# Two layers of a hybrid decoder: other PSUM banks for the first unit, outputs before gate products, and splits at other places

## The chip, the core and the metric

The kernel runs on one core of a Trainium2 chip, as one launch. The metric is the device time of a run in microseconds (us). The kernel before takes 1011.71 us, the median of three runs from 1011.68 to 1012.67.

## The reference, cut to what matters

256 tokens of 1024 channels go through two layers. Each layer adds half a SwiGLU, then a mixer, then half a SwiGLU. The mixer of the first layer is a diagonal state-space layer (S5), that of the second is block attention (MoBA; with 256 tokens, one block, it is causal attention). All is float32.

```python
def swiglu(h, w_gate, w_up, w_down):
    return (jax.nn.silu(h @ w_gate) * (h @ w_up)) @ w_down          # D_FF = 2816

def s5_mixer(h, ...):
    u = (h @ w_in)
    ...                                    # y: output of the linear recurrence over u, plus d_skip * u
    g = jax.nn.gelu(y)
    g = g * jax.nn.sigmoid(g @ w_glu)
    return g @ w_out

for layer in range(2):
    h = h + 0.5 * swiglu(rms_norm(h, ffn_norm[layer, 0]), ...)
    h = h + mixer[layer](rms_norm(h, mix_norm[layer]))
    h = h + 0.5 * swiglu(rms_norm(h, ffn_norm[layer, 1]), ...)
```

## The kernel before

**Phases.** The six phases run one after another on one stream of weights: `f00`, `s5`, `f01`, `f10`, `moba`, `f11`. `ffn` (L414) is `f00`, `ffn_w` (L513) the other three SwiGLUs.

**Products.** Each float32 product is made of three products of parts: a value is split into a high part (`whi`, `xh`) and the low rest (`wlo`, `xl`), and TensorE sums high x high, high x low and low x high into one bank of PSUM (`mm3`, L377 to L380; in `ffn_w` L531 to L533; in `glu` L1059 to L1061). The activations' parts are the tile `xa`.

**The weight stream** (`Stream`, L36). The weights come in units of 128 x 2048 float32, loaded by SP's queue into three raw buffers. A unit has two halves. `split` (L72) makes the high part of the next half on ScalarE (L81, with the norm's gain L87) and the low part on VectorE (L82, with gain L88, two pieces of 512 each); after the second half the raw buffer is free, and the load of the unit three places on is issued. There are nine slots for split halves (`HB`). `pump(n)` splits up to n halves if a slot and a raw buffer are there; `get` splits on the spot what is not split yet; `release` gives a slot back.

**The order of work is the order of the program.** Every engine runs its instructions in the order in which the Python code emits them (`manual_schedule`), and waits at each for its semaphores. So the place of a `pump` in the code is the place of the split in ScalarE's and VectorE's queues.

**PSUM.** Eight banks: two named pM (`psM`, sums of the gate and up products), two named pR (`psR`, transposes and small sums), and pA0 to pA3 (`psA`, the four sums of the down products; in S5 also the sums of the gate products, `glu`, and of the output products, `so`). A bank is taken again once the last reader of its tile before is done.

**f00.** For each of eleven units j of 256 columns, `gu(j, t)` makes gate and up sums of token tile t (eight steps k, of three products each), `gated` (L457) takes the Silu of the gate half on ScalarE into `sg`, pumps, and multiplies on VectorE into `act` (L463); `tr` transposes `act` (L476), `dn` adds to the down sums. The first unit, `gu0` (L438), goes through k with both token tiles in turn, since the inputs still arrive, and has its two sums in the two pM banks. The next unit's `gu(1, 0)` takes a pM bank again.

**S5.** `w_in` makes u in four parts. Then, for each of eight groups b: `t1` (L967) products, `rot` on VectorE (complex rotation and two scans) and GpSimd (L996 to L999), which gives `hr`; `y_out(b)` (L1016) sums the outputs in a pR bank, Gelu on ScalarE (`yg`, L1030), two transposes on VectorE (`gs`, L1033); `g_tr(b)` (L1036) transposes on TensorE into a pR bank, from which ScalarE and VectorE write the parts of g (low part L1046); `glu(b)` (L1048) adds group b's part of g @ w_glu to the four pA banks and pumps at set places. Within the last `glu`, `gate(i)` (L1069) takes the sigmoid (L1072), multiplies (L1074) and makes high and low parts (L1076, L1077). `so(b, t, n)` are the output products, `boundary` (L354) ends them, with `finish` (L352) adding the sums to h and `prep` transposing and splitting h for the next phase (L314, L316, L317). The last `prep` of a phase stands in the next one, at step k = 2 of its first unit (`entry_hooks`).

The loop that the change touches, with the groups' order (L1098):

```python
for b in range(3, NB):
    glu(b - 3)
    y_out(b)
    if b + 3 < NB:
        t1rot(b + 3)
    g_tr(b - 1)
```

Of the kernel before, what the change touches and what calls it, by code (L numbers as in the profile page):

```python
# [10 lines left out]
F32 = mybir.dt.float32  # L11
# [104 lines left out]
def trunk_kernel(ctx: ExitStack, tc, x, ffn_norm, ffn_w_gate, ffn_w_up, ffn_w_down, mix_norm,  # L116
# [10 lines left out]
    fp = ctx.enter_context(tc.tile_pool(name="ffn", bufs=2))  # L127
# [3 lines left out]
    def psM():  # L131
        return pp.tile([128, 512], F32, name="pM", tag="M", bufs=2)

    def psR():
        return pp.tile([128, 512], F32, name="pR", tag="R", bufs=2)

    def psA(i):
        return pp.tile([128, 512], F32, name=f"pA{i}", tag=f"A{i}", bufs=1)
# [129 lines left out]
    st = Stream(nc, units, rp, hp)  # L268
# [108 lines left out]
    def mm3(o, xh, xl, wh, wl, start, stop):  # L377
        mm(o, xh, wh, start=start, stop=False)  # L378
        mm(o, xh, wl, start=False, stop=False)  # L379
        mm(o, xl, wh, start=False, stop=stop)  # L380
# [33 lines left out]
    def ffn(tag, nxt, hooks, fill):  # L414

        V = nc.vector
        acc = [None] * 4
        AT, AC = {}, {}

        def gu(j, t, hooks):  # L420
            us = [where[tag, "g", j, a] for a in range(2)]
            ps = psM()
            ts = slice(t * 128, t * 128 + 128)
            for k in range(8):
                for fn in hooks.get(k, ()):
                    fn()
                fill(0.7)
                wh, wl = st.get(us[k // 4], (k % 4) // 2)
                c = slice((k % 2) * 512, (k % 2) * 512 + 512)
                mm3(ps, X["h"][:, k, ts], X["l"][:, k, ts], wh[:, c], wl[:, c], k == 0, k == 7)  # L430
                if k % 2:
                    if k < 7 and (j, t, k) != (L, 1, 5):
                        st.pump()
                    if t == 1:
                        st.release(us[k // 4], (k % 4) // 2)
            gated(j, t, ps)

        def gu0():  # L438

            us = [where[tag, "g", 0, a] for a in range(2)]  # L440
            pt = [psM() for t in range(2)]
            for q in range(4):
                u = us[q // 2]
                for t in range(2):
                    for f in hooks.get((q, t), ()):
                        f()
                    ts = slice(t * 128, t * 128 + 128)
                    for k in (2 * q, 2 * q + 1):
                        fill(0.7)
                        wh, wl = st.get(u, q % 2)  # L450
                        c = slice((k % 2) * 512, (k % 2) * 512 + 512)
                        mm3(pt[t], X["h"][:, k, ts], X["l"][:, k, ts], wh[:, c], wl[:, c], k == 0, k == 7)
                st.release(u, q % 2)
            for t in range(2):
                gated(0, t, pt[t])

        def gated(j, t, ps):  # L457
            sg = fp.tile([128, 256], F32, name="sg", bufs=1)
            nc.scalar.activation(sg, ps[:, 0:256], AF.Silu, scale=Rr[t])
            if (j, t) != (L, 1):  # L460
                st.pump()
            AC[t] = fp.tile([128, 256], F32, name="act", bufs=2)
            V.scalar_tensor_tensor(AC[t], ps[:, 256:512], Rr[t], sg, op0=OP.mult, op1=OP.mult)  # L463

        def tr(j, t):
            if t == 0:
                AT[j] = []
                for i, n in enumerate(("ah", "al")):
                    o = AO[2 * i + j % 2]
                    a2 = fp.tile([128, 640], F32R, name=n, bufs=2)  # L470
                    AT[j].append(a2[:, o:o + 512].rearrange("p (f c) -> p f c", c=256))
            ps = psR()
            pv = ps[:, 0:256].rearrange("p (f c) -> p f c", c=128)
            a = AC.pop(t)
            for f in range(2):
                nc.tensor.transpose(pv[:, f, :], a[:, f * 128:(f + 1) * 128], ident)  # L476
            ah, al = (x[:, :, t * 128:t * 128 + 128] for x in AT[j])
            nc.scalar.activation(ah, pv, AF.Copy)
            V.tensor_tensor(al, pv, ah.bitcast(F32), op=OP.subtract)

        def dn(j, f):
            u = where[tag, "d", j]
            for t in range(2):
                for n in range(2):
                    if j == 0 and f == 0:
                        acc[2 * t + n] = psA(2 * t + n)
                    bank_mm(acc, t, n, *AT[j], u, [f], j == 0 and f == 0, False)
                    fill(0.7)
                if t == 1:
                    st.release(u, f)  # L490
                st.pump()

        L = NJ - 1
        for j in range(NJ):
            if j == 0:
                gu0()
                continue
            gu(j, 0, {3: [lambda: tr(0, 0)], 6: [lambda: tr(0, 1)]} if j == 1 else {6: [lambda: tr(j - 1, 1)]})
            if j > 1:
                dn(j - 2, 1)  # L500
            gu(j, 1, {6: [lambda: tr(j, 0)]})
            if j:
                dn(j - 1, 0)

        def part(j, f):
            return lambda t, n: bank_mm(acc, t, n, *AT[j], where[tag, "d", j], [f], False, (j, f) == (L, 1))

        boundary(nxt, [part(L - 1, 1), part(L, 0), part(L, 1)], acc, 0.5, lambda: tr(L, 1))
        st.release(where[tag, "d", L - 1], 1)
        for i in range(2):  # L510
            st.release(where[tag, "d", L], i)
# [429 lines left out]
    def s5(nxt, entry):  # L941
# [65 lines left out]
        def t1rot(b):  # L1007
            t1ld(b)
            rot_ld(b)
# [6 lines left out]
        def y_out(b):  # L1016
            tb = TB.pop(b)
            v2 = tb[:, 0:1024].rearrange("p (i q c) -> p i q c", i=2, c=128)
            v3 = tb[:, 1024:1536].rearrange("p (q c) -> p q c", c=128)
            ps = psR()  # L1020
            hr = H.pop(b)
            for q in range(4):
                o = ps[:, q * 64:(q + 1) * 64]
                mm(o, v3[:, q, :], U[:, 4 * b + q, :, :], start=True, stop=False)
                mm(o, v2[:, 0, q, :], hr[:, 0, q, :], start=False, stop=False)
                mm(o, v2[:, 1, q, :], hr[:, 1, q, :], start=False, stop=True)
            if b + 3 < NB:
                ld_b(b + 3)
            yg = wp.tile([128, 4, 2, 32], F32, name="yg", bufs=1)
            nc.scalar.activation(yg.rearrange("p q t c -> p (q t c)"), ps[:, 0:256], AF.Gelu_apprx_tanh)  # L1030
            gs = wp.tile([128, 2, 4, 32], F32, name="gs", bufs=2)
            for t in range(2):
                V.transpose(gs[:, t], yg[:, :, t, :])  # L1033
            GS[b] = gs
# [13 lines left out]
        def glu(b, after=None):  # L1048

            u = where["glu", b // 2]  # L1050
            if b == 0:
                for i in range(4):
                    acc[i] = psA(i)
            gh, gl = GT["h"][:, b, :], GT["l"][:, b, :]
            wh, wl = st.get(u, b % 2)
            for o in range(8):
                d = acc[o // 2][:, (o % 2) * 256:(o % 2) * 256 + 256]
                c = slice(o * 128, o * 128 + 128)
                mm(d, wh[:, c], gh, start=b == 0 and o % 2 == 0, stop=False, skip_group_check=True)  # L1059
                mm(d, wh[:, c], gl, start=False, stop=False, skip_group_check=True)  # L1060
                mm(d, wl[:, c], gh, start=False, stop=b == NB - 1, skip_group_check=True)  # L1061
                if o == 7:
                    st.release(u, b % 2)
                if o == 3 and b < 7 or o == 7 and b in (5, 6):
                    st.pump()
                if after is not None and o % 2 == 1:
                    after(o // 2)
# [28 lines left out]
        t1rot(5)  # L1096
        g_tr(1)
        for b in range(3, NB):  # L1098
            glu(b - 3)
            y_out(b)  # L1100
            if b + 3 < NB:
                t1rot(b + 3)
            g_tr(b - 1)
# [8 lines left out]
        for b in range(2):  # L1112
            for t in range(2):
                for n in range(2):
                    so(b, t, n)
                if t == 1:
                    for i in range(2):
                        st.release(where["so", b], i)
                st.pump()
            st.pump()  # L1120

        boundary(nxt, [lambda t, n: so(2, t, n), lambda t, n: so(3, t, n, True)], acc, 1.0)
        for b in (2, 3):
# [171 lines left out]
    def fill(dt):  # L1295
        slot[0] += dt
        if slot[0] > 9.0:
            next(tab, None)
# [123 lines left out]
```

## Time and profile before

| | |
|---|---|
| runs | 1011.68, 1011.71, 1012.67 us |
| the profiled execution's own time | 1011.32 us |
| its span, from the first to the last instruction | 1009.5 us |
| mean granted TensorE clock | 0.998 |
| VectorE busy | 707.0 us (70%) |
| ScalarE busy | 574.4 us (57%) |
| GpSimd busy | 167.3 us (17%) |
| f00 | to about 228 us |
| S5 | about 228 to 335 us |
| f01's first unit and first down products | about 335 to 360 us |

In rows of the timeline, the first number is the start in us from the start of the span, the second the length in us; then engine, line, operation, `out<-in`, shapes, and the count of instructions merged into the row. In brackets stands how long the engine was idle before the row and what released it. Rows of the waits give engine, tile and line that waited, who released it, the total in us, how often, and the longest. A row of the windows gives a stretch and its length, the busy time of each engine with its instructions, the granted clock (1.00 is full), the DMA engines' share and GB/s.

### The profile page before, as it was taken

What the parts mean: (1) busy time and instruction counts of PE and PEld (TensorE: products, weight loads), DVE (VectorE), ACT (ScalarE), POOL (GpSimd) and SP (SyncE); (2) the same over time, 40 slices, a digit from 0 to 9 for tenths busy, and PEclk for the clock granted to TensorE, in tenths of its full rate; (3) what the DMA queues carried; (4) which work ended last, traced back from release to release, by engine and by line L of the source; (5) the groups of instructions that cost most, each with busy time, mean ns of one, the idle gap of its engine ahead of it and who ended that gap; (6) DMA issues with size and microseconds to landing.
All of it is one profiled execution on the core that took longest, in us unless ns stands there. A gap on an engine that the chain in (4) does not pass through costs nothing.

```text
span 1009.5 us, 16571 instructions
## 1 busy us (share of the span) xinstructions
PE 993.0 (98%) x6393; PEld 889.0 (88%) x6393; DVE 707.0 (70%) x1144; ACT 574.4 (57%) x1040; POOL 167.3 (17%) x330
## 2 busy tenths in 40 slices
PE   8999999999999999999999999999999999999998
PEld 6788888888997889999989999999888899999997
DVE  4799676857967677666657766666689667766662
ACT  5656778744335656555546555553788655555551
POOL 4981222113740100000000000000342010000000
PEclk9999999999999999999999999999999999999999
DMA  8886776876735467565626665645354456656531
GB/s 258 231 271 225 240 255 216 280 294 234 269 117 196 139 211 248 168 208 168 208 84 209 235 222 169 208 168 172 117 164 139 159 173 210 223 195 208 169 126 42
DMA packets 137535, 197.59 MB, mean 196 GB/s; under 512 B 16288, under 2 KB 109040, under 8 KB 137200
## 3 DMA queue, kind: packets, MB, share of 16 engines
q1 hardware_dynamic: 133088, 183.16, 54.6%
q0 software_dynamic: 3616, 12.66, 3.2%
q8 instruction: 50, 0.82, 0.3%
q10 hardware_dynamic: 752, 0.71, 0.3%
q14 instruction: 29, 0.24, 0.1%
HBM read 182.84 MB, written 13.66 MB: 195 GB/s over the span
## 4 chain that ended last, share of the span: by engine, by line
PE 87%; DVE 5%; issue 3%; POOL 2%; ACT 2%; ACTq 0%; POOLq 0%; DVEq 0%
PE pM L533 12%; PE pM L531 12%; PE pM L532 12%; PE pA L379 9%; PE pA L380 9%; PE pA L378 9%; PE pM L378 5%; PE pM L379 5%; PE pM L380 5%; DVE wlo L82 1%; PE pR L314 1%; POOL qrs L287 1%; PE pR L863 1%; DVE zo L992 1%; PE pR L843 1%
## 5 line engine op out<-in xcount | busy, mean ns | idle before, releaser
L531 PE MATMUL pM<-xa,whi 128*128 128x256 f32 x1056 | 295.7, 280 | 1.9 <-ACT whi L87 1.9
L533 PE MATMUL pM<-xa,wlo 128*128 128x256 f32 x1056 | 294.8, 279 | 0.3 <-DVE wlo L88 0.3
L532 PE MATMUL pM<-xa,whi 128*128 128x256 f32 x1056 | 294.8, 279 | 0.0
L88 DVE SCALAR_TENSOR_TENSOR wlo<-raw,gT,whi 128x512 fp32r<-128x512 f32 x328 | 228.0, 747 | 71.2 <-ACT whi L87 71.1
L82 DVE TENSOR_TENSOR wlo<-raw,whi 128x1024 fp32r<-128x1024 f32 x156 | 193.0, 1252 | 57.5 <-ACT whi L81 56.2
L87 ACT ACTIVATE whi<-raw,gT 128x512 fp32r<-128x512 f32 x328 | 213.5, 711 | 19.1 <-PE pA L380 14.1
L531 PEld LDWEIGHTS pM<-xa,whi 128*128 128x128 f32 x1056 | 198.5, 188 | 4.4 <-ACT whi L87 2.1
L532 PEld LDWEIGHTS pM<-xa,whi 128*128 128x128 f32 x1056 | 198.5, 188 | 2.5
L533 PEld LDWEIGHTS pM<-xa,wlo 128*128 128x128 f32 x1056 | 198.5, 188 | 0.5 <-DVE wlo L88 0.5
L81 ACT ACTIVATE whi<-raw 128x1024 fp32r<-128x1024 f32 x156 | 160.9, 1054 | 21.1 <-DMA raw<-in_ffn_w_up_dram 6.1
L378 PE MATMUL pA<-whi,ah 128*128 128x512 f32 x352 | 138.9, 395 | 0.3 <-ACT whi L81 0.3
L379 PE MATMUL pA<-wlo,ah 128*128 128x512 f32 x352 | 137.8, 391 | 0.8 <-DVE wlo L82 0.8
L380 PE MATMUL pA<-whi,al 128*128 128x512 f32 x352 | 137.7, 391 | 0.0
L378 PE MATMUL pM<-whi,xa 128*128 128x512 f32 x304 | 126.5, 416 | 2.3 <-DVE act L463 1.9
L546 ACT ACTIVATE sg<-gr 128x256 f32<-128x256 f32 x66 | 27.6, 418 | 165.4 <-DVE gr L543 165.4
L379 PE MATMUL pM<-wlo,xa 128*128 128x512 f32 x304 | 119.8, 394 | 1.7 <-DVE wlo L82 1.6
L380 PE MATMUL pM<-whi,xa 128*128 128x512 f32 x304 | 119.7, 394 | 0.0
L329 POOL TENSOR_TENSOR ms<-ss 128x1 f32<-128x1 f32 x10 | 1.9, 194 | 479.5 <-ACT sq L326 479.5
L380 PEld LDWEIGHTS pA<-whi,al 128*128 128x128 f32 x352 | 66.1, 188 | 14.3
L379 PEld LDWEIGHTS pA<-wlo,ah 128*128 128x128 f32 x352 | 66.2, 188 | 12.4 <-DVE wlo L82 1.1
L378 PEld LDWEIGHTS pA<-whi,ah 128*128 128x128 f32 x352 | 66.1, 188 | 12.0 <-ACT whi L81 0.5
L543 DVE TENSOR_TENSOR gr<-pM,rrow 128x512 f32<-128x512 f32 x66 | 45.5, 689 | 39.8 <-PE pM L533 39.7
(248 smaller groups left out, 1264.1 us busy)
## 6 DMA issues: line engine op xcount, KB each, us to landing
raw<-in_ffn_w_down_dram SPq DMA_DIRECT2D x44, 1024.0 KB, 5.1
raw<-in_ffn_w_gate_dram SPq DMA_DIRECT2D x80, 512.0 KB, 3.7
raw<-in_ffn_w_up_dram SPq DMA_DIRECT2D x80, 512.0 KB, 4.9
raw<-in_moba_w_qkv_dram SPq DMA_DIRECT2D x12, 1024.0 KB, 5.1
TB<-dB SPq DMA_DIRECT2D x8, 768.0 KB, 6.4
raw<-in_ffn_w_gate_dram SPq DMA_DIRECT2D x16, 256.0 KB, 4.5
raw<-in_ffn_w_up_dram SPq DMA_DIRECT2D x16, 256.0 KB, 4.7
dB<-tt POOLq DMA_DIRECT2D x16, 256.0 KB, 5.1
```

What stands on the lines that cost most here:

```text
L81: nc.scalar.activation(hi, r, AF.Copy)
L82: nc.vector.tensor_tensor(lo, r, hi.bitcast(F32), op=OP.subtract)
L87: nc.scalar.activation(hi[:, c], r[:, c], AF.Identity, scale=g)
L88: nc.vector.scalar_tensor_tensor(lo[:, c], r[:, c], g, hi[:, c].bitcast(F32), op0=OP.mult, op1=OP.subtract)
L378: mm(o, xh, wh, start=start, stop=False)
L379: mm(o, xh, wl, start=False, stop=False)
L380: mm(o, xl, wh, start=False, stop=stop)
L531: mm(o, a, xh, start=k == 0 and i == 0, stop=False, skip_group_check=True)
L532: mm(o, a, xl, start=False, stop=False, skip_group_check=True)
L533: mm(o, b, xh, start=False, stop=k == 7, skip_group_check=True)
L543: V.tensor_tensor(gr, ps.rearrange("p (i c) -> p i c", i=2), Rr["row"][:, None, :].to_broadcast([128, 2, 256]), op=OP.mult)
L546: nc.scalar.activation(sg, gr[:, 0, :], AF.Silu)
```

## The change

Three things are changed; what is computed stays the same.

- In f00's first unit the two sums go to the banks pA0 and pA2 in place of pM's. The two gated rows follow each other without a split between, and two splits follow them. `sg` becomes a part of a tile of 512 columns with two buffers, under the tag of the tile `gr`.
- In S5's loop `y_out(b)` stands ahead of `glu(b - 3)`.
- `glu` pumps a second time at b = 3, 4, 5 in place of 5, 6. In the first two blocks of `so`, each token tile is followed by `pump(2)`, in place of `pump()` with one more `pump()` at the end of the block.

```diff
@@ gu0
-            pt = [psM() for t in range(2)]
+            pt = [psA(2 * t) for t in range(2)]
...
             for t in range(2):
-                gated(0, t, pt[t])
-
-        def gated(j, t, ps):
-            sg = fp.tile([128, 256], F32, name="sg", bufs=1)
+                gated(0, t, pt[t], 0)
+            st.pump(2)
+
+        def gated(j, t, ps, pumps=1):
+            sg = fp.tile([128, 512], F32, name="sg", tag="gr", bufs=2)[:, 0:256]
             nc.scalar.activation(sg, ps[:, 0:256], AF.Silu, scale=Rr[t])
             if (j, t) != (L, 1):
-                st.pump()
+                st.pump(pumps)
             AC[t] = fp.tile([128, 256], F32, name="act", bufs=2)
             V.scalar_tensor_tensor(AC[t], ps[:, 256:512], Rr[t], sg, op0=OP.mult, op1=OP.mult)
@@ glu
-                if o == 3 and b < 7 or o == 7 and b in (5, 6):
+                if o == 3 and b < 7 or o == 7 and b in (3, 4, 5):
                     st.pump()
@@ s5
         for b in range(3, NB):
+            y_out(b)
             glu(b - 3)
-            y_out(b)
             if b + 3 < NB:
                 t1rot(b + 3)
             g_tr(b - 1)
@@ s5, the blocks of so
                 if t == 1:
                     for i in range(2):
                         st.release(where["so", b], i)
-                st.pump()
-            st.pump()
+                st.pump(2)
```

## The prediction

> **What bounds the kernel now.** I read the page's first part, then the waits of TensorE, then the clock by stretches, then the timelines of TensorE, ScalarE and VectorE round each long wait that the change touches.
>
> ```profile
> PE 993.0 (98%) x6393; PEld 889.0 (88%) x6393; DVE 707.0 (70%) x1144; ACT 574.4 (57%) x1040; POOL 167.3 (17%) x330
> ```
>
> ```profile
> PE pM L378 <- DVE act L463: 1.9, 1, 1.9
> PE pM L531 <- ACT whi L87: 1.9, 1, 1.9
> ...
> PE pA L379 <- DVE wlo L82: 1.1, 2, 0.8
> PE pA L378 <- DVE xa L1076: 1.0, 1, 1.0
> ...
> PE pA L1060 <- DVE xa L1046: 0.9, 1, 0.9
> ```
>
> TensorE is busy for 98% of the span, and the change alters no product. It can win only what TensorE stands still or runs slow. The five rows are that: 6.8 us, at five places, all of them in the first unit of f00, in S5's second half and in the first units of f01.
>
> A wait costs more than its bracket, which counts from a modelled end. These rows give the difference:
>
> ```profile
> 309.31 0.28 PE L1060 MATMUL pA<-xa,whi 128*128 128x256 f32 x1
> 309.43 0.28 PE L1061 MATMUL pA<-xa,wlo 128*128 128x256 f32 x1
> 310.73 0.47 PE L378 MATMUL pA<-whi,xa 128*128 128x512 f32 x1 [1.02 <-DVE xa L1076]
> ...
> 317.94 0.50 PE L379 MATMUL pA<-wlo,xa 128*128 128x512 f32 x1 [0.35 <-DVE wlo L82]
> ```
>
> Starts are 0.12 us apart, lengths are 0.28: each product overlaps the next by 0.16 us, and a wait loses that overlap too. So 310.73 lost 1.18 us and 317.94 lost 0.51. (A 512-column product takes twice the 0.12, 0.23 us, and its 0.39 overlaps by the same 0.16.)
>
> **Part 1, f00's first unit: sums in pA, gated rows ahead of the splits.**
>
> ```profile
> 24.28 0.40 PE L380 MATMUL pM<-whi,xa 128*128 128x512 f32 x1
> 26.62 0.47 PE L378 MATMUL pM<-whi,xa 128*128 128x512 f32 x1 [1.94 <-DVE act L463]
> 26.93 0.46 PE L379 MATMUL pM<-wlo,xa 128*128 128x512 f32 x1
> ```
>
> ```profile
> 23.40 0.47 ACT L459 ACTIVATE sg<-pM,rr 128x256 f32<-128x256 f32 x1 [2.10 <-PE pM L380]
> 23.77 1.05 ACT L81 ACTIVATE whi<-raw 128x1024 fp32r<-128x1024 f32 x1
> ```
>
> ```profile
> 24.85 1.23 DVE L82 TENSOR_TENSOR wlo<-raw,whi 128x1024 fp32r<-128x1024 f32 x1 [1.82 <-ACT whi L81]
> 26.00 0.47 DVE L463 SCALAR_TENSOR_TENSOR act<-pM,rr,sg 128x256 f32<-128x256 f32 x1
> ```
>
> Now the next unit waits for a bank of pM, which the gated row of t = 0 frees at 26.47, since it stands on VectorE behind the split's low part. With the sums in pA that wait is gone. But the same edit moves the split that unit 1 needs for k = 0 and 1 behind both Silus on ScalarE, and the second Silu waits for TensorE's last product: 24.28 + 0.40 = 24.68, read about 0.1 later. One instruction of ScalarE follows the Silu by 23.77 - 23.40 = 0.37. So the high part starts at 24.78 + 0.37 = 25.15 and ends at 26.20 (1.05), the low part runs from 26.23 to 27.46 (1.23). TensorE starts one product at 26.25 and stops again: the second takes the low part, at 27.5 where it was 26.93. The stall is not removed, it is 0.57 us longer, with a new cause. Behind the waiting product stands all of unit 1. What the wait then does to the clock is the unknown:
>
> ```profile
> 24.00:26.70 2.70, 0.76 (x4) 0.32 (x4) 1.62 (x2) 0.93 (x2) 2.25 (x6) 1.00 1.09 256
> 26.70:30.50 3.80, 3.80 (x10) 2.57 (x11) 2.46 (x3) 2.25 (x3) 3.32 (x7) 0.55 0.17 18
> ```
>
> After the idle 1.94 us the granted clock is 0.55 for 3.8 us: ten products in 3.80, 0.38 each where 0.23 is usual, a loss of 1.5 us. After the change TensorE idles 1.57 + 0.8 us with one product between, more than now, so I take the slow stretch to stay and set +0.5 us (the start shifts by 0.57, and a slow stretch that ends at a fixed time would give a tenth back). Were it to go, the part would be worth 0.57 - 1.5 = -0.9. Bounds: -0.9 to +0.6.
>
> The Trainium skill (TensorE: Matmul & The Clock Gate, section "Why this matters for your kernels") asks for no idle gaps over about 3 us between bursts and says that one idle window takes the clock back to half. By that rule neither 1.94 us now nor the two shorter gaps after would cost clock. The trace shows 0.55 after 1.94 us, so I follow the row; what the rule would give is the second rival.
>
> The pA banks are free in time: the entry's transposes use them, and the down products' first write comes two units later. The tile sg moving to two larger buffers adds no instruction. I set both at nothing; the cover is those two units, and without it the down products' first write would wait up to the 0.47 us of a gated row.
>
> **Part 2, the loop of S5: y_out(b) ahead of glu(b - 3).**
>
> ```profile
> 267.25 0.36 PE L1059 MATMUL pA<-xa,whi 128*128 128x256 f32 x1
> 268.55 0.38 PE L1060 MATMUL pA<-xa,whi 128*128 128x256 f32 x1 [0.94 <-DVE xa L1046]
> ```
>
> Today glu(0) issues one product and waits for g_tr(0)'s low part (L1046). The outputs put there instead seem to fill that hole, but y_out(3) takes its sums in one of the two banks of pR, and the last two were given to g_tr(0) and g_tr(1): it needs g_tr(0)'s, whose last reader is the same L1046. So TensorE waits until 268.55 all the same, and the one product that it did ahead (0.2 us to the next start) is done later: +0.2. Bounds: +0.1 to +0.3. In the later rounds no wait stands now, and the order of rounds is unchanged. VectorE gets each round's transposes of yg ahead of the split in place of behind it, which shifts rot(6) and rot(7) by about 0.1. On SP the loads of TB now go ahead of the raw loads. All are needed rounds later: nothing.
>
> **Part 3, pumps.** In glu the extra pumps sit at b = 3, 4, 5 in place of 5, 6, so there is one more; each block of so pumps four in place of three. No split is added, they come earlier. Counting the calls: all four halves of the first two so units are split ahead of the gates (three now), and at f01's start four of its halves are ready in place of one.
>
> ```profile
> 306.09 1.99 ACT L81 ACTIVATE whi<-raw 128x1024 fp32r<-128x1024 f32 x2
> 307.98 1.07 ACT L1072 ACTIVATE sg<-pA 128x512 f32<-128x512 f32 x2
> ```
>
> ```profile
> 307.16 2.36 DVE L82 TENSOR_TENSOR wlo<-raw,whi 128x1024 fp32r<-128x1024 f32 x2 [1.82 <-ACT whi L81]
> 309.44 0.68 DVE L1074 TENSOR_TENSOR gf<-gf,sg 128x512 f32<-128x512 f32 x1
> 310.16 0.43 DVE L1076 CAST xa<-gf 128x512 fp32r<-128x512 f32 x1
> 310.62 0.69 DVE L1077 TENSOR_TENSOR xa<-gf,xa 128x512 fp32r<-128x512 f32 x1
> ...
> 316.67 5.76 DVE L82 TENSOR_TENSOR wlo<-raw,whi 128x1024 fp32r<-128x1024 f32 x5
> ```
>
> (a) At the gates two splits stand ahead of gate(0). With one of them gone (2.36 / 2 = 1.18 on VectorE), gate(0) starts at 308.3, its cast ends at 309.5, its low part at 310.2. TensorE ends glu(7) at 309.55, so its first two products run and the third waits a few hundredths: -1.14 of the 1.18.
> (b) The second half of so(1) is one of the five splits from 316.67 on, and 317.94 waited for it. It is done ahead of the gates now: -0.51.
> (c) The start of f01:
>
> ```profile
> 336.31 0.60 PE L314 MATMUL pR<-cst,h 128*128 128x128 f32 x4
> 338.81 0.38 PE L531 MATMUL pM<-xa,whi 128*128 128x256 f32 x1 [1.91 <-ACT whi L87]
> ...
> 339.60 0.38 PE L533 MATMUL pM<-xa,wlo 128*128 128x256 f32 x1 [0.29 <-DVE wlo L88]
> ```
>
> ```profile
> 337.58 0.69 DVE L317 TENSOR_TENSOR xa<-pR,xa 128x512 fp32r<-128x512 f32 x1 [1.16 <-ACT xa L316]
> ```
>
> The second half of f01's first unit is split only when TensorE asks for it, behind prep(1, 1) on ScalarE. These waits cost 1.91 + 0.29 + 2 x 0.16 = 2.52. Split before, they go; late next is prep itself: the products for k = 4 would come at 336.75 + 12 x 0.12 = 338.2, and their low part of x ends at 338.27. I leave 0.1: -2.4.
> (d) The first down products:
>
> ```profile
> 355.21 0.28 PE L533 MATMUL pM<-xa,wlo 128*128 128x256 f32 x1
> 355.75 0.50 PE L378 MATMUL pA<-whi,ah 128*128 128x512 f32 x1 [0.26 <-ACT whi L81]
> 357.01 0.50 PE L379 MATMUL pA<-wlo,ah 128*128 128x512 f32 x1 [0.76 <-DVE wlo L82]
> ```
>
> Starts at 355.33 and 355.56 without waits, at 357.01 with them: 1.45 lost, because the down weights' split comes late. Three halves ahead, it is done a unit sooner: -1.45. Further on both orders run into the nine slots and pump alike, so nothing more is won.
>
> What hides the extra splits: three more halves (six low parts of 0.7 us) stand on VectorE between the gates and the end of so, where this row shows it idle for 3.13 us:
>
> ```profile
> 326.89 0.69 DVE L352 SCALAR_TENSOR_TENSOR h<-pA,h 128x512 f32<-128x512 f32 x1 [3.13 <-PE pA L380]
> ```
>
> ```profile
> raw<-in_ffn_w_up_dram SPq DMA_DIRECT2D x16, 256.0 KB, 4.7
> ```
>
> The gates end 1.1 earlier, one split is out, so four so splits end at 320.4 and eight half parts of 0.69 at 325.9. The finish (L352) comes due at 326.89 - 1.14 - 0.51 + 0.2 = 325.4. It is up to 0.5 late, and TensorE has other products of so to do meanwhile: nothing, up to 0.5.
>
> **The sum:** 0.5 + 0.2 - 1.14 - 0.51 - 2.4 - 1.45 = -4.8 us. The profiled execution took 1011.32 (span 1009.5 and 1.8 round it), which gives 1006.5; the median of the runs lies 0.4 above it: 1006.9.
>
> **Rivals.**
> 1. As forecast, but the clock holds in f00 (the rule above). For it: 2.4 us of idle is cut in two by a product. Against it: a single gap of 1.94 sufficed. 1006.9 - 1.4 = 1005.5.
> 2. The stalls at f01's start only move. Were the early splits in so to cost as much at the finish and at prep as they save, (c) and (d) would be gone: 1011.7 + 0.5 + 0.2 - 1.65 = 1010.8, which is no change. For it: the finish is already at the edge. Against it: the idle 3.13 us. Half of it is a case of its own: 1008.8.
> 3. Slower, by the queue: the second raw of f01 can be loaded only when so(2)'s second half is split, at 318.05, four transfers over 1.4 us, each landing 4.7 us on: 324.2, high parts to 325.5, low parts to 326.2. VectorE is in order, so the finish stands behind a wait for this DMA, and with it the boundary. Beyond a landing of about 4.4 us each us costs one. It decides from a landing of 4.4 + 4.8 = 9.2 us on; at 12 us the time is 1006.9 + 7.6 = 1014.5. For it: the low parts do stand ahead of the finish. Against it: 4.7 is the median of sixteen.
>
> **How the numbers follow.** Forecast 0.54 (own range 1006.0 to 1007.8), clock holds 0.15, half of rival 2 0.13, rival 2 0.11, rival 3 0.07. About 0.2%, 2 us, is what a measurement tells from no change: faster 0.82, same 0.11, slower 0.07. The range runs from the clock's case less 0.6, 1004.9, to the half case plus 0.8, 1009.6.
>
> **What would show it.** Part 1: the wait of the first L378 in pM names ScalarE's high part, and a second wait in L379 names the low part; the clock round 27 to 30 us decides the first rival. Part 2: the wait on L1046 stands at an L1024. Part 3: no wait on L1076, on L87 at f01's start or on the first down weights. It is wrong if finishes in S5's boundary wait, or if the waits at f01 keep their length.

## The result, and the profile after

| | us, median | lowest to highest | runs |
|---|---|---|---|
| before | 1012.6 | 1011.41 to 1014.65 | 8 |
| changed | 1008.93 | 1008.61 to 1010.5 | 8 |

The ratio is 0.9964, 95% interval 0.9953 to 0.9975: 0.36% faster, 3.7 us, where 4.8 were forecast. The profiled execution of the changed kernel was the slowest of its eight, 1010.5 us with a span of 1008.7, so its trace shows a smaller gain than the runs; what is dear in it is the clock, as the rows below show. Lines 456 to 1119 have moved down by one, so L1046 is now L1047.

First TensorE's waits in the changed kernel: engine, tile and line that waited, who released it, us in total, how often, the longest.

```profile
PE pA L379 <- DVE wlo L82: 1.6, 2, 0.8
PE pM L378 <- ACT whi L81: 1.5, 1, 1.5
PE pR L1025 <- issue: 1.1, 1, 1.1
...
PE pM L379 <- DVE wlo L82: 0.9, 2, 0.8
PE pR L314 <- DVE h L352: 0.8, 1, 0.8
```

Gone are the waits on the gate's cast (L1076), on the high part at f01's start (L87) and those of f01's down products. The row pA L379 is gu0's own waiting for its first weights, which stood under pM before and now goes under the bank's new name. New are three: the high and low part in pM (part 1), y_out (L1025) and a finish (L352).

f00's first unit, TensorE's timeline and the stretch after it (busy time by engine, then granted clock, DMA share, GB/s):

```profile
26.20 0.50 PE L378 MATMUL pM<-whi,xa 128*128 128x512 f32 x1 [1.51 <-ACT whi L81]
27.46 0.69 PE L379 MATMUL pM<-wlo,xa 128*128 128x512 f32 x1 [0.76 <-DVE wlo L82]
```

```profile
26.70:30.50 3.80, 3.04 (x7) 2.38 (x8) 3.12 (x3) 1.34 (x2) 3.49 (x5) 0.62 0.31 30
```

The two waits name the two parts of one split, at 26.20 and 27.46, and the mean clock of the stretch after them is 0.62.

S5's loop, TensorE and VectorE, and the clock by stretches:

```profile
267.75 0.39 PE L1043 MATMUL pR<-cst,gs 128*128 128x128 f32 x2
269.24 0.41 PE L1025 MATMUL pR<-U,TB 128*128 128x64 f32 x2 [1.10 <-issue]
...
278.00 1.89 PE L968 MATMUL pM<-U,TA 128*128 128x64 f32 x16
```

```profile
268.76 0.38 DVE L1047 TENSOR_TENSOR xa<-pR,xa 128x256 fp32r<-128x256 f32 x1
```

```profile
269.00:272.00 3.00, 2.76 (x16) 2.79 (x17) 2.97 (x7) 0.00 (x0) 2.92 (x4) 0.66 0.47 195
272.00:275.00 3.00, 3.00 (x16) 3.00 (x16) 2.77 (x6) 0.97 (x2) 1.72 (x2) 0.50 0.43 101
275.00:278.00 3.00, 3.00 (x20) 3.00 (x20) 2.34 (x3) 0.66 (x2) 2.92 (x3) 0.70 0.67 250
```

y_out(3) starts right after L1047 ends (268.76 + 0.38 = 269.14): it waits for the bank that g_tr(0) holds. The profile names no releaser here ("issue"); the reader has to find it by the times and the code, and `best_p2` below bears it out. Then the clock is at half from 269.95 to 276.78 us, by the trace's own record of it. That was not in the forecast.

S5's boundary: the last issue of the load, then ScalarE, VectorE and TensorE.

```profile
323.42 0.47 SPq L170 DMA_DIRECT2D raw<-in_ffn_w_up_dram  x1
```

```profile
325.68 1.34 ACT L87 ACTIVATE whi<-raw,gT 128x512 fp32r<-128x512 f32 x2 [3.90 <-DMA raw<-in_ffn_w_up_dram]
328.44 1.34 ACT L87 ACTIVATE whi<-raw,gT 128x512 fp32r<-128x512 f32 x2 [1.42 <-DMA raw<-in_ffn_w_up_dram]
```

```profile
329.20 1.41 DVE L88 SCALAR_TENSOR_TENSOR wlo<-raw,gT,whi 128x512 fp32r<-128x512 f32 x2 [0.99 <-ACT whi L87]
330.53 1.28 DVE L352 SCALAR_TENSOR_TENSOR h<-pA,h 128x512 f32<-128x512 f32 x2
```

```profile
331.27 0.66 PE L314 MATMUL pR<-cst,h 128*128 128x128 f32 x4 [0.80 <-DVE h L352]
```

The last high parts start at 328.44, 5.0 us after the load's last issue. The high parts wait for the load, the low parts for them, and the finish stands behind them on VectorE; the first two finishes then run back to back (x2), and TensorE waits 0.80 us.

### The profile page after: what moved, and what is told of

Its sections match the earlier page's. It is cut to its first block, busy times and chain, and to the rows that moved or that the text cites. A ratio compares the mean times of both kernels' runs of the same rounds, so it can differ in the third digit from the quotient of the medians.

```text
span 1008.7 us, 16569 instructions
## 1 busy us (share of the span) xinstructions
PE 995.6 (99%) x6393; PEld 892.6 (88%) x6393; DVE 704.7 (70%) x1144; ACT 574.9 (57%) x1040; POOL 165.2 (16%) x330
## 4 chain that ended last, share of the span: by engine, by line
PE 90%; DVE 3%; POOL 2%; DMA 2%; issue 2%; ACT 1%; SPq 0%; DVEq 0%; POOLq 0%; ACTq 0%
PE pM L532 12%; PE pM L533 12%; PE pM L534 12%; PE pA L378 9%; PE pA L379 9%; PE pA L380 9%; PE pM L378 5%; PE pM L379 5%; PE pM L380 5%; PE pR L314 1%; POOL qrs L287 1%; PE pR L864 1%; PE pR L1027 1%; PE pR L1026 1%; PE pR L1025 1%
## 5 line engine op out<-in xcount | busy, mean ns | idle before, releaser
L87 ACT ACTIVATE whi<-raw,gT 128x512 fp32r<-128x512 f32 x328 | 213.5, 711 | 19.4 <-PE pA L380 14.1
L379 PE MATMUL pA<-wlo,ah 128*128 128x512 f32 x352 | 137.7, 391 | 0.0
L378 PE MATMUL pM<-whi,xa 128*128 128x512 f32 x288 | 119.9, 416 | 1.5 <-ACT whi L81 1.5
L379 PE MATMUL pM<-wlo,xa 128*128 128x512 f32 x288 | 113.4, 394 | 0.9 <-DVE wlo L82 0.9
L380 PE MATMUL pM<-whi,xa 128*128 128x512 f32 x288 | 113.5, 394 | 0.0
L379 PEld LDWEIGHTS pA<-wlo,ah 128*128 128x128 f32 x352 | 66.2, 188 | 11.3
```

The source lines that it names most:

```text
L87: nc.scalar.activation(hi[:, c], r[:, c], AF.Identity, scale=g)
```

## The experiments

Eleven kernels, in three batches: p1_only to p1_p3, fill_y3 to best, and the last three of the table. The first batch ran on another chip than the other two, and in each the kernel before was timed beside them (medians 1012.1, 1012.47 and 1012.51 us). Ratios are to the kernel before of the same batch, with their 95% intervals.

| label | what it is | us, median | ratio |
|---|---|---|---|
| p1_only | part 1 alone | 1012.1 | 1.0001 [0.9993, 1.001] |
| p2_only | part 2 alone | 1015.18 | 1.0032 [1.0021, 1.0043] |
| p3_only | part 3 alone | 1006.37 | 0.9943 [0.9931, 0.9955] |
| p1_p3 | changed kernel without part 2 | 1005.21 | 0.9938 [0.9926, 0.995] |
| fill_y3 | changed kernel, products in the stop ahead of y_out(3) | 1007.13 | 0.9943 [0.993, 0.9957] |
| early_u1 | parts 1, 3, unit 1's splits earlier | 1003.07 | 0.9904 [0.9889, 0.992] |
| no_last | parts 1, 3 without so's last two pumps | 1008.5 | 0.9953 [0.9938, 0.9968] |
| best | parts 1, 3 with three mends | 1001.44 | 0.989 [0.9874, 0.9905] |
| glu_pumps | glu's pumps alone | 1008.13 | 0.9952 [0.9938, 0.9966] |
| so_pumps | so's pumps alone | 1007.51 | 0.9948 [0.9936, 0.9961] |
| best_p2 | best with part 2 | 1001.61 | 0.989 [0.9877, 0.9904] |

### Each part alone, and the changed kernel without part 2

The edits are the hunks of the change: `p1_only` has those of gu0 and gated, `p2_only` that of S5's loop, `p3_only` those of glu and so, `p1_p3` all but that of the loop.

> The kernel before with part 1 alone (pA banks and gated rows ahead of the splits in f00's first unit). Theory: the stall ahead of unit 1 stays, 0.5 us longer, its second half now on the low part of the split, and the slow clock after it stays: +0.5 us, about 1.0005 of before. Rival (the bank was the bound, and the clock holds): -0.9 us, the clock round 27 to 30 us at 1.00.

> The kernel before with part 2 alone (y_out(b) ahead of glu(b - 3)). Theory: y_out(3) waits for g_tr(0)'s bank, about 1.1 us on L1046, and the longer stop, with none of glu's products in it, takes the clock down in S5 for one or two stretches of 3.4 us: +0.2 for the wait and 1.7 to 3.4 for the clock, +1.9 to +3.6 us, granted clock of 270 to 277 us well under 1.00. Rival: the slow clock in the changed kernel is no result of this order (it comes and goes in either): +0.2 us and clock 1.00 here.

> The kernel before with part 3 alone (pumps). Theory: no waits at the gates, in so(1) and at f01's first unit and down products (-5.5 us), and a new one where the first finish stands behind splits that wait for their load (+1.2): -4.3 us or somewhat more. Rival (the pumps carry no more than the whole change does): -3.7 us, with the other two parts at nothing.

> The changed kernel without part 2 (glu(b - 3) ahead of y_out(b) as before). Theory, that part 2 costs the clock: faster than the changed kernel by 1.9 to 3.6 us, that is -5.5 us or more against before, and clock 1.00 in S5. Rival, that part 2 costs only its wait: -3.9 us against before.

Part 2 alone is slower by 0.32%, 3.2 us. TensorE's wait and the clock in its profile:

```profile
PE pR L1024 <- issue: 1.1, 1, 1.1
```

```profile
270.00:274.00 4.00, 4.00 (x22) 4.00 (x21) 3.96 (x6) 0.35 (x2) 2.65 (x3) 0.53 0.41 133
```

Without part 2, the same stretch of the kernel with parts 1 and 3 has a clock of 1.00, and the wait is glu's of 0.9 us:

```profile
PE pA L1061 <- DVE xa L1047: 0.9, 1, 0.9
PE pR L314 <- DVE h L352: 0.5, 1, 0.5
```

```profile
270.00:274.00 4.00, 4.00 (x39) 4.00 (x37) 4.00 (x5) 0.69 (x2) 2.72 (x4) 1.00 0.24 67
```

So theory held for part 2, and its rival (the clock comes and goes in either order) fell. The two waits shown for p1_p3 are all that it has between 255 and 362 us. Part 3 saves 0.57%, 5.8 us (4.6 to 7.0); the rival of 3.7 lies outside its interval, but so does the 4.3 that the theory named as the least. A part of the 5.8 may not be part 3's: it does not touch f00, where the clock falls in some executions, and four of its five runs have a mean clock of 0.999 or 1.000, where all eighteen of the kernel before in that batch have 0.996 to 0.998. The phases at the end of the experiments set it at 4.8. Part 1 alone cannot be told from nothing: the interval holds the +0.5 us and reaches down to -0.7.

The forecast's unknown for part 1, the clock after the stop, turned out to differ from execution to execution. With f00 as before, part 3's profile shows the stop of 1.95 us and no slow clock:

```profile
26.88 0.47 PE L378 MATMUL pM<-whi,xa 128*128 128x512 f32 x1 [1.95 <-DVE act L463]
```

```profile
26.70:30.50 3.80, 2.86 (x12) 2.02 (x13) 2.23 (x4) 2.37 (x3) 3.24 (x8) 1.00 0.18 18
```

Counted over the profiles of this study: the stop as before took the clock down in three of five (before, p2_only, glu_pumps; not in p3_only, so_pumps), part 1's stop in four of five (the changed kernel, p1_only, fill_y3, no_last; not in p1_p3).

The traces show what goes with it. The clock on record is 1.00 or 0.50 and nothing between (0.62 is a mean over a stretch), and within a trace all its changes stand whole multiples of 3.41 us apart, as on a grid of steps. In the kernel before one step runs from 23.70 to 27.11 us and holds the whole stop, and the next step is at half:

```profile
23.70:27.11 3.41, 1.47 (x7) 0.94 (x6) 1.62 (x2) 1.64 (x4) 2.81 (x8) 1.00 1.08 251
27.12:30.53 3.41, 3.41 (x9) 2.23 (x8) 2.49 (x3) 1.83 (x2) 3.02 (x6) 0.50 0.07 9
```

In p1_p3 the grid lies elsewhere. It cuts the stop at 25.36 us, and the clock holds:

```profile
25.36:28.78 3.42, 1.85 (x7) 1.33 (x8) 2.96 (x4) 2.65 (x3) 3.02 (x5) 1.00 0.62 63
28.78:32.19 3.41, 3.41 (x18) 2.58 (x16) 2.46 (x3) 2.40 (x4) 3.10 (x5) 1.00 0.72 194
```

A step's length less TensorE's busy time is its empty time. In the seven profiles where the clock fell in f00, the step before held 1.9 to 2.3 us of it; in the three where it held, no step of the stop had more than 1.6. Kernels with the same code up to there have the grid at other places, so its place does not come from that code. Why the clock stayed down for two steps in one of the seven (glu_pumps) and for one in the others is not shown.

### Is it the empty time that takes the clock?

```diff
         for b in range(3, NB):
+            if b == 3:
+                ps = psA(0)
+                for _ in range(5):
+                    mm(ps[:, 0:128], ones, ones, start=True, stop=True)
             y_out(b)
```

> The changed kernel with five filler products (128 columns, into pA0, read by nobody) ahead of y_out(3), where TensorE stands empty. Theory: it is the empty 1.1 us that takes the clock down, so with the filler the clock of 270 to 277 us is 1.00 and the kernel comes to about 0.994 of before (-6 us), as without part 2 but for 0.2 us. Rival: the clock falls because y_out's products of 64 columns stand there in place of glu's; then it stays at 0.5 to 0.7 with the filler too, and the ratio at 0.9964 (-3.7 us).

```profile
267.94 1.28 PE L1103 MATMUL pA<-ones 128*128 128x128 f32 x10
269.20 0.41 PE L1025 MATMUL pR<-U,TB 128*128 128x64 f32 x2
...
274.82 1.45 PE L968 MATMUL pM<-U,TA 128*128 128x64 f32 x12
```

```profile
270.00:274.00 4.00, 4.00 (x37) 4.00 (x37) 3.97 (x6) 1.63 (x3) 2.70 (x3) 1.00 0.52 167
```

y_out(3) starts when it did (269.20 against 269.24), but the clock stays at 1.00, and the next t1 starts after 5.62 us where the changed kernel's took 278.00 - 269.24 = 8.76. In that execution the same work took 3.14 us longer, with 6.83 us of it at half clock. Five products of no use (each shows as two instructions, as y_out's do) make the kernel faster, 0.9943 against 0.9964 (the two intervals overlap by a hair, from 0.9953 to 0.9957). The mean clock of every run agrees: 0.994 to 0.996 in the eight runs of the changed kernel, 0.997 to 0.999 in the six with the filler, 0.998 to 1.000 in the five of p1_p3. The products of 64 columns are not the cause by themselves, since they run at 1.00 once the stop ahead of them is filled.

That the empty time alone is the cause is not shown. These are the changed kernel's steps of the clock round the stop:

```profile
266.54:269.95 3.41, 2.31 (x22) 2.10 (x21) 3.41 (x10) 1.39 (x5) 2.13 (x3) 1.00 1.05 416
269.95:276.78 6.83, 6.83 (x34) 6.83 (x34) 6.17 (x9) 1.63 (x3) 5.39 (x6) 0.50 0.45 142
```

Here 1.10 us empty in a step was enough (in p2_only too), while p1_p3's step in f00 held 1.57 and the clock stayed. The work in the two steps differs: products of 64 and 128 columns here, of 512 there. So the stop is needed for the fall, and what else in the step counts stays open.

### The stop in f00: splits ahead of the gated rows

```diff
                 st.release(u, q % 2)
+                if q == 2:
+                    st.pump(2)
             for t in range(2):
                 gated(0, t, pt[t], 0)
-            st.pump(2)
```

> Parts 1 and 3, with the two splits for unit 1 moved from behind the gated rows to the third of gu0's four steps, where ScalarE waits. Theory: part 1 won nothing because the splits stood behind both Silus; with them ahead, TensorE goes from gu0 into unit 1 without a stop, which is worth 1.51 + 0.76 + 2 x 0.16 = 2.6 us against parts 1 and 3, and up to 1.5 more in the executions where the clock fell after the stop: 0.9938 of before becomes 0.990 to 0.992. Rival: the loads bound this stage (DMA busy 0.98 of 34 to 60 us), TensorE waits for a later unit in its place: 0.9938 stays.

```profile
21.17 1.99 ACT L81 ACTIVATE whi<-raw 128x1024 fp32r<-128x1024 f32 x2
23.32 0.48 ACT L461 ACTIVATE sg<-pA,rr 128x256 f32<-128x256 f32 x1
```

```profile
24.20 0.39 PE L380 MATMUL pA<-whi,xa 128*128 128x512 f32 x1
24.42 0.39 PE L378 MATMUL pM<-whi,xa 128*128 128x512 f32 x1
```

ScalarE stood idle from 21.3 to 23.4 in the kernel before; the two high parts fit there, and TensorE goes from gu0 (pA) into unit 1 (pM) without a stop. 0.9904 against 0.9938: 3.4 us, as the theory had it, and the rival of a bound by the loads fell. In the profiles f00 ends 2.2 us earlier than in p1_p3, whose clock held there too; the theory's 2.6 was for that case.

### The finish behind the splits

```diff
-                st.pump(2)
+                if (b, t) != (1, 1):
+                    st.pump(2)
```

> Parts 1 and 3 without the last two pumps of so (the second half pair of f01's first unit). Theory: the first finish waits because it stands on VectorE behind low parts whose load lands late; without them its wait (0.5 us in the run with parts 1 and 3, and what the clock makes of it) is gone, but unit 0 of f01 then waits at k = 4 for the split, about 1.3 us: 0.6 to 0.8 us slower than parts 1 and 3. Rival: the first unit's later halves are not late even so, as in the kernel before: 0.7 us faster.

```profile
PE pA L379 <- DVE wlo L82: 0.8, 1, 0.8
PE pM L532 <- ACT whi L87: 0.5, 1, 0.5
PE pM L534 <- DVE wlo L88: 0.3, 1, 0.3
PE pA L378 <- ACT whi L81: 0.2, 1, 0.2
```

The finish no longer waits, but f01 does, at its first unit and at its first down products. The direction is the theory's. The size is 0.0015 or 1.5 us where 0.6 to 0.8 were expected; the intervals of the two kernels overlap, but from the end of f00 to that of f01 the profiles differ by 2.1 us. The down products' wait, which the theory left out, came back too.

### Glu's pumps and so's pumps apart

> The kernel before with the changed pumps of glu alone (second pump at b = 3, 4, 5). Theory: terms (a) and (b) are theirs: no wait on L1076 (-1.14) and none on the low part in so(1) (-0.51), and the later splits come one half earlier, which shortens the wait at f01's start too: -1.7 to -3 us, 0.997 to 0.9983 of before. Rival: what is saved at the gates comes back in so and at f01's start: 0.999 to 1.000.

> The kernel before with the changed pumps of so alone (pump(2) after each token tile). Theory: terms (c) and (d) are theirs: no wait on L87 at f01's start (-2.4) and none at the first down products (-1.45), less what the finish waits: -3 to -3.8 us, 0.9962 to 0.997 of before, with the waits on L1076 and in so(1) as before. Rival: without the glu pumps the splits stand so late that the finish waits longer than is saved: 0.998 to 1.000.

TensorE's waits from 255 to 362 us, first with glu's pumps alone, then with so's alone:

```profile
PE pA L1060 <- DVE xa L1046: 0.9, 1, 0.9
PE pA L379 <- DVE wlo L82: 0.8, 1, 0.8
PE pM L531 <- ACT whi L87: 0.5, 1, 0.5
PE pM L533 <- DVE wlo L88: 0.3, 1, 0.3
PE pA L378 <- ACT whi L81: 0.2, 1, 0.2
```

```profile
PE pA L378 <- DVE xa L1076: 1.0, 1, 1.0
PE pA L1060 <- DVE xa L1046: 0.9, 1, 0.9
PE pA L379 <- DVE wlo L82: 0.4, 1, 0.4
PE pR L314 <- DVE h L352: 0.2, 1, 0.2
```

Each takes away the waits that were put to it: glu's pumps those of the gates and of so(1), so's pumps those of f01. The times say more than the waits: 4.9 and 5.3 us where 1.7 to 3 and 3 to 3.8 were expected, though together they are worth 5.8. The wait at f01's start falls from 1.9 to 0.5 with glu's pumps alone, which explains part of it, since either pair cures most of that wait. From the end of f00 to that of f01 the profiles give 3.2 and 3.6 us, and 4.8 for both together, close to what was expected. What the medians show beyond that lies outside these two phases and is not settled; in this batch the kernel before lay at 1012.39 to 1014.54, and the intervals, about 1.4 us to either side, reach to 3.4 and 3.9.

### A faster version

`best` is parts 1 and 3 with early_u1's edit, with one of the last two pumps in place of both or none, and with g_tr(0) ahead of rot(4); `best_p2` is that with part 2.

```diff
-                st.pump(2)
+                st.pump(1 if (b, t) == (1, 1) else 2)
...
-        t1rot(4)
-        y_out(2)
-        g_tr(0)
+        t1ld(4)
+        g_tr(0)
+        rot_ld(4)
+        y_out(2)
```

> Parts 1 and 3, with the early splits of early_u1, one of the last two pumps left out, and g_tr(0) emitted ahead of rot(4), so that its low part does not stand behind rot(4) and glu(0) need not wait. Theory: -2.6 to -4.1 (f00), -0.5 (finish), -1.1 (L1046) against parts 1 and 3: 0.988 to 0.990 of before. Rival: loads in f00 and VectorE in S5 take the gain back: 0.993.

> The fastest kernel so far with part 2 put back (y_out(b) ahead of glu(b - 3)). Theory: part 2 costs only because y_out(3) meets a bank that g_tr(0) holds, and the clock falls in that stop; with g_tr(0) ahead of rot(4) the bank is free and part 2 is worth nothing either way: 0.989 of before, clock 1.00. Rival: the order itself costs: 0.991 or more.

All that TensorE waits for between 255 and 362 us in `best`:

```profile
PE pR L1026 <- ACT yg L1032: 0.2, 1, 0.2
```

`best` takes 0.989 of before, 1.1%; `best_p2` the same. With the bank free in time, y_out ahead of glu costs nothing and brings nothing.

### The phases, from the profiles

A phase ends with its fourth finish (L352 in the kernel before). The table gives where f00 ends and how long S5 and f01 take, in us. After f01 all these profiles take the same, 483.7 to 483.8 us.

| kernel | f00 ends at | clock in f00 | S5 | f01 |
|---|---|---|---|---|
| before | 226.40 | fell | 108.95 | 190.50 |
| p1_only | 227.00 | fell | 108.97 | 190.55 |
| p2_only | 226.96 | fell | 112.38 | 190.55 |
| p3_only | 226.19 | held | 108.27 | 186.41 |
| p1_p3 | 225.39 | held | 107.81 | 186.40 |
| changed | 227.03 | fell | 111.60 | 186.40 |
| glu_pumps | 227.92 | fell, for two steps | 107.11 | 189.15 |
| so_pumps | 225.86 | held | 109.44 | 186.40 |
| no_last | 226.80 | fell | 107.17 | 189.15 |

Part 2 costs 3.4 us of S5 (p2_only against before), as much as 6.83 us at half clock lose, and 3.8 in the changed kernel against p1_p3, whose finish waits 0.3 us less. Part 3 saves 4.1 us of f01. In S5 it saves 1.8 us where no finish waits (glu_pumps, no_last), and 0.7 and 1.1 where one does (p3_only, p1_p3). In f00 the same code ends anywhere from 225.86 to 227.92, by the clock.

## Why the prediction came out as it did

- **Part 1** was read rightly in its mechanism: the stop stays, with TensorE's first product at 26.20 (forecast 26.25) and the second at 27.46 (27.5). The size, +0.5, lies in an interval of -0.7 to +1.0 us. In the profiles f00 ends 0.4 to 0.6 us later than in the kernel before's where the clock fell, and 1.0 earlier where it held (forecast +0.5 and -0.9), but with f00 as before its end moves by as much from execution to execution. What was taken as fixed there, the slow clock, depends on where the clock's steps fall.
- **Part 2** is where the prediction failed. It found that y_out(3) would meet g_tr(0)'s bank and wait for the same L1046, and priced that at "+0.2" with bounds of +0.1 to +0.3, as if a stop cost only its own length. Part 2 alone cost 3.2 us (2.1 to 4.4), and taking it out of the changed kernel won 2.6 (0.9964 to 0.9938). The stop grew from 0.94 us, with a product of glu ahead of it, to 1.10 with none, and the clock was at half for the next 6.83 us, a loss of 3.4; fill_y3 shows that without the stop it holds. The prediction had the row for this in hand (clock 0.55 after 1.94 us) and used it in f00 alone.
- **Part 3** was forecast at 1.14 + 0.51 + 2.4 + 1.45 = 5.5 us. All four waits are gone, and by the phases they were worth 1.8 us in S5 (forecast 1.65) and 4.1 in f01 (3.85), less what a finish waits. The tenth that was left for prep is not to be seen.
- **The finish** was forecast to come up to 0.5 us late at no cost. It cost a wait of 0.80 in the changed kernel's profile (0.9 and 0.5 in p3_only and p1_p3), and by the phases 0.7 to 1.1 us. The prediction had named a waiting finish as a sign that it was wrong, and here it was. This is the third rival's mechanism, with 5.0 us from the last issue to the high part where the prediction had 4.7; what was wrong is the slack given to TensorE there.
- **The sum** of -4.8 against -3.7 came nearer than its terms, and part of that is luck. In the two profiles the phases moved by +0.6 in f00, +2.65 in S5 and -4.1 in f01, -0.8 in all, where the terms were +0.5, -1.45 and -3.85: S5 was missed by 4.1 us, part 2's clock and the finish. The medians are kinder, since the changed kernel's profiled run was its slowest, 1.6 us above its median, and the kernel before's was 1.3 below its own. Its other runs have a mean clock of 0.995 or 0.996 against 0.994, so they lost less to the clock; at which place, no trace shows. The measured time lies inside the range, between the forecast and the case of half a gain at f01, but not for that rival's reason.

The Trainium skill (TensorE: Matmul & The Clock Gate, section "Why this matters for your kernels") allows idle gaps up to about 3 us. The traces disagree: 1.10 us sufficed in both profiles that had that stop. Its other statement, in the section on the HAM clock gate, that the window of activity is free-running and so its place against the kernel is a matter of chance, agrees with f00, where like stops met either clock and the steps of 3.41 us lay at other places from execution to execution.

## What to carry to other kernels

Price a stop of TensorE twice: for its length, and for the clock that it may take, here for 3.41 or 6.83 us after it; on this kernel, 98% TensorE, the second was 3.4 us where the first had been priced at 0.2. When work is moved into a hole, list every resource that the moved work needs (here a PSUM bank) and look for the releaser that made the hole: if it is the same one, the hole stays. And move splits or copies on an in-order engine only up to the point where their loads have landed; past it, everything behind them waits too.

## What the hardware showed that was not expected

- A stop of 1.10 us took the granted clock to 0.50 for 6.83 us (269.95 to 276.78 in the changed kernel), in both profiles that had it. The stop of 0.94 to 0.96 us in the same place, with one product of glu ahead of it, left it at 1.00 in all eight profiles that had it. Where between the two it turns was not tried, and no stop of 1.10 us was met that a step of the clock cuts in two.
- The same stop of 1.94 to 1.97 us in f00 was followed by half clock in three executions and by full clock in two. It fell where one step of 3.41 us held the whole stop, and held where the grid cut it.
- A part of the spread of a kernel's runs goes with the clock: p1_p3's runs took 1004.97 to 1005.21 us at a mean clock of 0.999 or 1.000, and 1007.16 and 1007.21 us at 0.998. No trace of the latter two shows where they lost it.
